# Modulation sums, query projections and inverse-transform quarters reordered around a 2-D attention stage, with a bias table that holds the mask

## Chip, core and metric

The kernel runs on one core of one Trainium2 chip. The metric is device time in microseconds of one execution. All times here are of that core: runs of the whole kernel, and one execution recorded by the hardware profiler, with its trace.

## What is computed

Two layers of a diffusion backbone over 512 tokens of width 1024, with 256 context tokens. Layer 0 mixes with a Hyena long convolution (512 channels) beside 2-D neighbourhood attention (8 heads of 64), layer 1 with a Conformer convolution; after each comes a ConvFFN of width 2816. Every sub-layer sits between RMS norms whose scale, shift and gate come from a conditioning vector (`m = silu(c) @ w_mod + b_mod`). The part that the change touches, cut from the reference:

```python
shift1, scale1, gate1, shift2, scale2, gate2 = adaln_params(c, w_mod[layer], b_mod[layer])
z = hn @ w_in[e]
y_hy = hyena_mixer(z[..., :3 * HY_WIDTH], ...)      # x0 * (irfft(rfft(x1*v) * k_f) + (x1*v) * bias)
q, k, v = jnp.split(z[..., 3 * HY_WIDTH:], 3, axis=-1)
...
s_loc = jnp.einsum('bjqhd,brjkhd->bhjqrk', q_blk, k_blk)     # 16 query columns x 8 rows of 32 key columns
s_loc = s_loc + bias.transpose(0, 2, 3, 1, 4)                # relative position table, per head
s_loc = jnp.where(col_ok[:, :, None, :], s_loc, NEG_BIG)     # -1e30 outside the window
s_ctx = jnp.einsum('bjqhd,bchd->bhjqc', q_blk, kc)
p = jax.nn.softmax(jnp.concatenate([s_loc, s_ctx], axis=-1), axis=-1)
y = jnp.concatenate([y_hy, y_na], axis=-1) @ w_out[e]
```

## The kernel before

Everything is fp32. A product of matrices is made of three matmuls on high and low parts (`mm3`, L296 to L299). Weights come by a stream: SP loads a tile of 128 x 1024 (512 KB) into one of three `raw` buffers (L308), ScalarE casts its high half (L314), VectorE subtracts for the low half (L315); the halves lie in `w` tiles, eight buffers. `s` tiles (31 buffers) hold nearly all else, and PSUM has eight banks (`ps`).

The program is written as one sequence, and a scheduler, which simulates a timeline as it builds, settles each engine's order from it; each engine then works strictly in its own order, and SP issues loads in its own.

The stages around the change, in layer 0:

- key projection: `k_proj` (L962), whose pieces kX and kcX are written by ScalarE and VectorE (L975, L976);
- forward transform: `fdft` (L982) makes four sums of products in PSUM (pv); its `prod` (L992) forms v0 and v1 (L998 to L1001), multiplies them by the filter K (one product on POOL, L1007, one on VectorE, L1008), combines (L1011, L1012) and splits the result into Eh and El (L1017, L1019). It runs twice;
- value projection: six accumulators va (L1045 on), copied to V; `v_shift` (L1072) copies shifted rows by DMA;
- inverse transform, in four quarters of 128 channels (py, L1081 on), each followed by two VectorE operations (L1096, L1098) that end in yh;
- query projection: `q_proj` (L1104), four of them; pz, then qX and qL (L1118, L1119);
- attention: 16 blocks u, four for each pair of heads. For each u the loop (L1224) calls scores (sc), exponent (L1172 on VectorE: score plus bias table BM, with the negative row maximum; then ScalarE), normalizing one block later (reciprocals on VectorE L1179, scaling on POOL L1180), transposes of P (pt) and their copies three blocks later, products with V (po) five later.

The bias table comes by `bm_load` (768 columns a head, L1131, with a memset of the context part, L1130), and `bm_make` adds the mask on POOL (L1135).

Beside this run background generators, of which `bg_step(n)` (L501) advances n steps wherever the code calls it. `mod_cols(0, (2,))` is one: it sums 16 tiles of `wcol`, each scaled by one number per partition, into `acc`, then eight small matmuls (pm, L465) reduce it to the second norm's scale and shift. With `side=True`, as here, ScalarE scales (L446) and POOL adds (L448); without it, VectorE does both in one operation (L452).

Of the kernel before, what the change touches and what calls it, by code (L numbers as in the profile page):

```python
# [29 lines left out]
def shape_constants():  # L30
    f64 = np.float64
    k = np.arange(256)
    t = np.arange(512)
    th = np.outer(2 * k + 1, 2 * t + 1) % 4096
    C = np.cos(th * (np.pi / 2048))
    S = np.sin(th * (np.pi / 2048))

    tf = np.zeros((4, P, 2, 256))
    for par in range(2):
        for hf in range(2):  # L40
            tt = 2 * (128 * hf + np.arange(128)) + par
# [36 lines left out]

    kb = [0, 8, 32]
    mask = np.zeros((P, 3, 4, 8, 8))  # L80
    s2, c8 = np.meshgrid(np.arange(2), np.arange(8), indexing="ij")
    for i, j in enumerate((0, 1, 3)):
        for s in range(2):
            for c in range(8):
                qc = 16 * j + 8 * s + c
                ws = min(max(qc - 8, 0), 48)
                kc = kb[i] + 8 * np.arange(4)[:, None] + np.arange(8)[None, :]
                ok = (kc >= ws) & (kc < ws + 16)
                m = np.where(ok, 0.0, -1e30)
                for r in range(8):  # L90
                    mask[s * 64 + r * 8 + c, i] = m[:, None, :]
    mask = mask.reshape(P, 768)

    kk = np.arange(128)
    w = np.pi * (2 * kk + 1) / 256
    tl = np.arange(256)
    ca = np.cos(np.outer(tl, w))
    sa = np.sin(np.outer(tl, w))
    f4 = np.zeros((4, P, 2, 128))
    for i, (lo, keep) in enumerate(((0, (0, 256)), (128, (0, 256)), (128, (0, 241)), (0, (15, 256)))):  # L100
        loc = lo + np.arange(128)
        on = ((loc >= keep[0]) & (loc < keep[1]))[:, None]
        f4[i, :, 0] = ca[loc] * on
        f4[i, :, 1] = sa[loc] * on
    f4 = f4.transpose(1, 0, 2, 3).reshape(P, 1024)
    i4 = np.zeros((4, P, 2, 128))
    for i, (lo, keep) in enumerate(((0, (0, 128)), (128, (0, 64)), (0, (64, 128)), (128, (0, 128)))):
        loc = lo + np.arange(128)
        on = ((np.arange(128) >= keep[0]) & (np.arange(128) < keep[1]))[None, :]
        i4[i, :, 0] = ca[loc].T * on / 128.0  # L110
        i4[i, :, 1] = sa[loc].T * on / 128.0
    i4 = i4.transpose(1, 0, 2, 3).reshape(P, 1024)
    j = np.arange(31)
    k31 = np.concatenate([np.cos(np.outer(j - 15, w)), np.sin(np.outer(j - 15, w))], 1)
    out = dict(tf=tf, ti=ti, cst=cst, zT=zT, dec=dec, qrow=q, mask=mask, f4=f4, i4=i4, k31=k31)
    return {n: np.ascontiguousarray(a.astype(np.float32)) for n, a in out.items()}


# [14 lines left out]
def layout(inp):  # L133
# [58 lines left out]
    a["fw3"] = g["hy_f_w3"][0]  # L192
    a["fw4"] = g["hy_f_w4"][0]

    rpb = g["na_rpb"][0]
    pad = np.concatenate([np.zeros_like(rpb[:, :, :17]), rpb, np.zeros_like(rpb[:, :, :17])], 2)
    tab = []
    for s in range(2):
        for r in range(8):
            for c in range(8):  # L200
                rows = pad[:, 7 - r:15 - r]
                per = []
                for off in (15, 7, -1):
                    b = 17 + off - (8 * s + c)
                    seg = rows[:, :, b:b + 32].reshape(8, 8, 4, 8).transpose(0, 2, 1, 3)
                    per.append(seg)
                tab.append(np.stack(per, 1))
    a["rpb"] = np.stack(tab, 1).reshape(8, P, 768)
    a.update(shape_constants())
    return {k: np.ascontiguousarray(v) for k, v in a.items()}, cols  # L210

# [41 lines left out]
def backbone_kernel(ctx: ExitStack, tc: tile.TileContext, a, cols, out, dump=None, stop=None, mark=lambda s: None):  # L253
# [76 lines left out]
    def flat(ap, pat):  # L330
        return ap.rearrange(pat)
# [96 lines left out]

    MOD = {}

    def gemv_acc(src, n, cs, init=None, side=False):
        rs = []

        def ld(k):
# [5 lines left out]
        for k in range(n):  # L440
            if k < n - 1:
                ld(k + 1)
            ck_ = cs[:, k:k + 1]
            if side:
                t_ = acc if k == 0 else s4(F32, (P, 1024), "gt")
                A.activation(t_, rs[k], AF.Copy, bias=0.0, scale=ck_)  # L446
                if k:
                    G.tensor_tensor(acc, acc, t_, op=ALU.add)  # L448
            elif k == 0 and init is None:
                V.tensor_scalar(acc, rs[k], ck_, None, op0=ALU.mult)  # L450
            else:
                V.scalar_tensor_tensor(acc, rs[k], ck_, init if k == 0 else acc, op0=ALU.mult, op1=ALU.add)  # L452
            yield acc

    def mod_cols(l, whichs, side=False):

        n = 2 * len(whichs)
        acc = None
        for acc in gemv_acc(a[f"wcol{l}"], 8 * n, scn[n], side=side):
            yield  # L460
        for _ in range(8):
            yield
# [488 lines left out]
                ctx_T()  # L951
        V.tensor_tensor(pp[i // 2][:, i % 2], got[0], got[1], op=ALU.mult)
    bg_drain()
    bg += [mod_cols(0, (2,), True)]


    mark("kproj")
# [24 lines left out]
    def fdft(fc):  # L982
# [9 lines left out]
        def prod():  # L992
# [10 lines left out]
            for pr, v in ((0, v0), (1, v1)):  # L1003
                kt = K[(fc, pr)]
                yy = s4(n="yy")
                tm = od if pr else s4(n="ytm")
                G.tensor_tensor(tm, v, kt[:, 1:2].broadcast_to([P, 2, 512]), op=ALU.mult)  # L1007
                V.tensor_tensor(yy, v, kt[:, 0:1].broadcast_to([P, 2, 512]), op=ALU.mult)  # L1008
                y.append((yy, tm))
            for yy, tm in y:  # L1010
# [9 lines left out]
            E[fc] = (eh, el)  # L1020
        return prod

    bg_step(3)
    ev0 = k_proj(0)
    p_T(3)
    bg_step(3)
    ev0()
    ev1 = k_proj(1)
    ev1()
    bg_step(3)  # L1030
    pr0 = fdft(0)
    pr0()
    mark("fdft")
    ev2 = k_proj(2)
    ev2()
    bg_step(3)
    ev3 = k_proj(3)
    ev3()
    bg_step(3)
    pr1 = fdft(1)  # L1040
    pr1()
    bg_step(3)


    mark("vproj")  # L1045
# [2 lines left out]
    for kp in range(4):  # L1048
# [11 lines left out]
                mm3(vacc[c], ah, al, wh[:, ns], wl[:, ns], kc == 0, kc == 7)  # L1060
        if kp in (1, 2):
            TI[kp - 1] = split(load(a["ti"][kp - 1]), None)
        bg_step(3)

    Vt = {}
    for c in range(6):
# [13 lines left out]

    mark("inv")  # L1081
    yh = [s4(n="yh") for _ in range(2)]
    for m in range(4):
        py = ps("py")
        ms = slice(m * P, (m + 1) * P)
        for par in range(2):
            o = py[:, par * 256:(par + 1) * 256]
            for fc in range(2):
                for cs in range(2):
# [6 lines left out]
        V.scalar_tensor_tensor(pi.rearrange("p (i e) -> p i e", e=2), pi.rearrange("p (i e) -> p i e", e=2),  # L1096
                               pc("hyb", m), py.rearrange("p (e i) -> p i e", e=2), op0=ALU.mult, op1=ALU.add)
        V.tensor_tensor(yh[m // 2][:, m % 2], pi, x0[m // 2][:, m % 2], op=ALU.mult)  # L1098

    mark("qproj")  # L1100

# [16 lines left out]
                A.mul(t_[HALF[r], e], src, 0.125)  # L1118
            V.scalar_tensor_tensor(l_[HALF[e], e], src, 0.125, f(t_[HALF[e], e]), op0=ALU.mult, op1=ALU.subtract)  # L1119

    q_proj(0)
    bg_step(1)

    mask = w4(F32, (P, 1024), "mask")
    SP.dma_start(mask[:, 0:768], a["mask"])
    BM = {}

    def bm_load(hd):
        BM[hd] = w4(F32, (P, 4, 256), "BM")
        G.memset(BM[hd][:, 3], 0.0)  # L1130
        SP.dma_start(flat(BM[hd][:, 0:3], "p a b -> p (a b)"), a["rpb"][hd])  # L1131

    def bm_make(hd):
        b = flat(BM[hd][:, 0:3], "p a b -> p (a b)")
        G.tensor_tensor(b, b, mask[:, 0:768], op=ALU.add)  # L1135

    for hd in range(2):
        bm_load(hd)
    q_proj(1)
    for hd in range(2):  # L1140
        bm_make(hd)
    bg_step(1)
    dmp("p", pT[0])
    dmp("x0", x0[0])
    dmp("yh", yh[0])

    mark("att")
    KS = (0, 1, 3, 4)
# [65 lines left out]
    def a_out(hp):  # L1214
# [5 lines left out]
        A.copy(hi, src)  # L1220
        V.tensor_tensor(lo, src, f(hi), op=ALU.subtract)

    DN, DT, DV = 1, 3, 5
    for u in range(16 + DV + 1):  # L1224
        if u < 16:
            a_scores(u)
            a_exp(u)
        if 2 <= u < 4:
            q_proj(u)
        if DN <= u < 16 + DN:  # L1230
            a_norm(u - DN)
        if DT <= u < 16 + DT:
# [3 lines left out]
            a_pv(u - DV)  # L1236
        if u > DV and (u - DV) % 2 == 0:
            a_out((u - DV) // 2 - 1)
        if u == 2:
            v_shift()  # L1240
        if u % 4 < 2 and u < 12:
            bm_load(u // 4 * 2 + u % 4 + 2)
        if u % 4 in (1, 2) and u < 12:
            bm_make(u // 4 * 2 + u % 4 + 1)
    dmp("yA", yA[0])
    mix.close()

# [302 lines left out]
```

## Time and profile before

| | us |
|---|---|
| median of 3 runs | 1291.08 |
| lowest and highest | 1290.09, 1294.53 |
| the profiled execution | 1290.61 |
| its span in the trace | 1288.8 |
| TensorE busy | 1249.9 (97%) |
| VectorE, ScalarE, POOL busy | 817.3 (63%), 526.8 (41%), 160.2 (12%) |

The mean granted clock of TensorE is 0.994 of full speed, and 171.00 MB move by DMA. The names of the trace are: PE for TensorE's matmuls, PEld for its weight loads, DVE for VectorE, ACT for ScalarE, POOL for GpSimd, SP for SyncE. Times in the trace count from the start of the span. A row "A <- B" in the list of waits says what an engine waited for, with the total, the number and the longest.

### The profile page before, as it was taken

To read this page: it belongs to the slowest core of one execution; us is meant where nothing else is said; L and a number is where in the kernel's file an instruction comes from. 1 tells how busy PE (TensorE), PEld (TensorE's weight loads), DVE (VectorE), ACT (ScalarE), POOL (GpSimd) and SP (SyncE) were. 2 spreads that over 40 slices of the span, in tenths; PEclk is the share of its full clock that TensorE was granted. 3 is DMA by queue.
4 is the path that set the end of the run, shared out by engine and by line. 5 is a ranking of instruction groups with operands and counts; after the bars stand their busy time and mean duration, and the time that the engine had idled before them with its cause. 6 is when DMAs were issued, how large, how long until landed. Compare 5 with 4: busy or idle time off the path is not lost.

```text
span 1288.8 us, 15592 instructions
## 1 busy us (share of the span) xinstructions
PE 1249.9 (97%) x6044; PEld 1027.3 (80%) x6044; DVE 817.3 (63%) x1068; ACT 526.8 (41%) x804; POOL 160.2 (12%) x198
## 2 busy tenths in 40 slices
PE   6999979999999999999999999999999999999997
PEld 3688867877898888878888887878888888888886
DVE  4577588476557888877825565686677555556233
ACT  5453543286435333243514433242544333345221
POOL 3210365283010000000000100101100000000001
PEclk9999998999999999999999999999999999999999
DMA  9536533342506477766336052040255333232321
GB/s 354 179 115 181 162 115 131 129 121 83 163 1 190 169 230 244 237 210 207 107 105 196 25 185 73 1 147 1 66 167 187 98 94 95 98 97 99 98 83 65
DMA packets 47818, 171.00 MB, mean 133 GB/s; under 512 B 5757, under 2 KB 5788, under 8 KB 47744
## 3 DMA queue, kind: packets, MB, share of 16 engines
q1 hardware_dynamic: 47092, 168.49, 39.9%
q0 software_dynamic: 464, 1.19, 0.4%
q8 instruction: 47, 0.77, 0.2%
q10 hardware_dynamic: 188, 0.33, 0.1%
q14 instruction: 27, 0.22, 0.1%
HBM read 167.10 MB, written 2.10 MB: 131 GB/s over the span
## 4 chain that ended last, share of the span: by engine, by line
PE 76%; DMA 8%; DVE 7%; ACT 4%; issue 3%; POOL 1%; SPq 0%; DVEq 0%; POOLq 0%; ACTq 0%
PE pz L297 12%; PE pz L298 12%; PE pz L299 12%; PE acc L297 8%; PE acc L298 8%; PE acc L299 8%; DMA raw<-in_wup 3%; DMA raw<-in_wcol 3%; DVE w L315 2%; PE pg L297 2%; PE pg L298 2%; PE pg L299 2%; ACT w L314 2%; PE po L1206 1%; PE pt L1186 1%
## 5 line engine op out<-in xcount | busy, mean ns | idle before, releaser
L299 PE MATMUL pz<-hTh,w 128*128 128x512 f32 (+1 forms) x920 | 345.2, 376 | 0.5 <-DVE w L315 0.5
L297 PE MATMUL pz<-hTh,w 128*128 128x512 f32 (+1 forms) x920 | 344.6, 377 | 0.9 <-DVE hTh L543 0.5
L298 PE MATMUL pz<-hTl,w 128*128 128x512 f32 (+1 forms) x920 | 345.4, 376 | 0.0
L315 DVE TENSOR_TENSOR w<-raw,w 128x1024 fp32r<-128x1024 f32 x159 | 201.1, 1268 | 211.1 <-ACT w L314 206.8
L314 ACT CAST w<-raw 128x1024 fp32r<-128x1024 f32 x159 | 166.3, 1051 | 345.5 <-PE pz L298 128.6
L299 PEld LDWEIGHTS pz<-hTh,w 128*128 128x128 f32 x920 | 173.8, 189 | 32.2 <-DVE w L315 1.0
L297 PEld LDWEIGHTS pz<-hTh,w 128*128 128x128 f32 x920 | 173.0, 189 | 31.5 <-DVE hTh L543 1.0
L298 PEld LDWEIGHTS pz<-hTl,w 128*128 128x128 f32 x920 | 173.9, 189 | 30.2 <-DVE hTl L544 0.4
L298 PE MATMUL acc<-w,gs 128*128 128x512 f32 x256 | 99.6, 389 | 0.0
L299 PE MATMUL acc<-w,gs 128*128 128x512 f32 x256 | 98.3, 389 | 0.0
L297 PE MATMUL acc<-w,gs 128*128 128x512 f32 x256 | 97.0, 389 | 0.0
L452 DVE SCALAR_TENSOR_TENSOR acc<-raw,sc,acc 128x1024 f32<-128x1024 f32 x59 | 75.6, 1281 | 28.6 <-DMA raw<-in_wgate 19.6
L416 POOL TENSOR_SCALAR t<-t,t 128x1 f32<-128x1 f32 x19 | 6.6, 348 | 636.6 <-ACT py L425 628.2
L901 ACT ACTIVATE cv<-pz,pk 128x512 f32<-128x512 f32 x88 | 67.6, 774 | 0.0
L903 DVE SCALAR_TENSOR_TENSOR cv<-pz,pk,cv 128x511 f32<-128x511 f32 x88 | 65.6, 747 | 1.8
L902 DVE SCALAR_TENSOR_TENSOR cv<-pz,pk,cv 128x511 f32<-128x511 f32 x88 | 65.2, 744 | 0.2 <-ACT cv L901 0.2
L1283 ACT ACTIVATE cv<-cv 128x512 f32<-128x512 f32 x44 | 27.7, 629 | 81.2 <-DVE cv L903 81.1
L297 PEld LDWEIGHTS acc<-w,gs 128*128 128x128 f32 x256 | 48.1, 188 | 10.1
L299 PEld LDWEIGHTS acc<-w,gs 128*128 128x128 f32 x256 | 48.1, 188 | 9.9
L298 PEld LDWEIGHTS acc<-w,gs 128*128 128x128 f32 x256 | 48.1, 188 | 9.9
L315 DVE TENSOR_TENSOR wk<-raw,wk 128x1024 fp32r<-128x1024 f32 x30 | 37.1, 1246 | 28.9 <-ACT wk L314 28.9
L558 DVE TENSOR_TENSOR py<-acc,gg 128x512 f32<-128x512 f32 x32 | 21.8, 688 | 48.4 <-ACT py L425 48.4
(334 smaller groups left out, 2050.2 us busy)
## 6 DMA issues: line engine op xcount, KB each, us to landing
raw<-in_wup SPq DMA_DIRECT2D x88, 512.0 KB, 3.6
raw<-in_wcol SPq DMA_DIRECT2D x48, 512.0 KB, 4.4
raw<-in_wdn SPq DMA_DIRECT2D x44, 512.0 KB, 3.6
raw<-in_wgate SPq DMA_DIRECT2D x32, 512.0 KB, 4.3
raw<-in_pw SPq DMA_DIRECT2D x24, 512.0 KB, 4.7
raw<-in_win SPq DMA_DIRECT2D x20, 512.0 KB, 3.6
land<-in_wmod SPq DMA_DIRECT2D x16, 512.0 KB, 10.2
raw<-in_wout SPq DMA_DIRECT2D x8, 512.0 KB, 3.6
```

The costliest lines, as they stand in the source:

```text
L297: PE.matmul(o, ah, bh, start=start, stop=False)
L298: PE.matmul(o, ah, bl, start=False, stop=False)
L299: PE.matmul(o, al, bh, start=False, stop=stop)
L314: A.copy(hi, r)
L315: V.tensor_tensor(lo, r, f(hi), op=ALU.subtract)
L452: V.scalar_tensor_tensor(acc, rs[k], ck_, init if k == 0 else acc, op0=ALU.mult, op1=ALU.add)
L558: V.tensor_tensor(p_[:, sl], y2[i], gg[:, sl], op=ALU.mult)
L901: A.activation(dst, pz, AF.Identity, bias=pc(bk, i), scale=pc(wk + "1", i))
L902: V.scalar_tensor_tensor(dst[:, 1:w], pz[:, 0:w - 1], pc(wk + "0", i), dst[:, 1:w], op0=ALU.mult, op1=ALU.add)
L903: V.scalar_tensor_tensor(dst[:, 0:w - 1], pz[:, 1:w], pc(wk + "2", i), dst[:, 0:w - 1], op0=ALU.mult, op1=ALU.add)
L1186: PE.transpose(b["pt"][:, c * P:(c + 1) * P], b["P"][:, c * P:(c + 1) * P], ident)
L1283: A.activation(cv[:, 0], cv[:, 0], AF.Silu, bias=0.0, scale=1.0)
```

## The change

Five things change. The second norm's modulation sums are made by VectorE, not by ScalarE and POOL. The product L1007 moves from POOL to VectorE. The calls of `bg_step` are fewer in the projections and transforms, and some stand in the inverse quarters and the attention loop. Query projections and inverse quarters take turns, the last two inside the first two rounds of the attention loop. The bias table is laid out on the host with the mask and the zeros of the context part, 1024 columns a head, so the mask's load, its sums and the memsets go.

```diff
-            if side:
-                t_ = acc if k == 0 else s4(F32, (P, 1024), "gt")
-                A.activation(t_, rs[k], AF.Copy, bias=0.0, scale=ck_)
-                if k:
-                    G.tensor_tensor(acc, acc, t_, op=ALU.add)
-            elif k == 0 and init is None:
+            if k == 0 and init is None:
                 V.tensor_scalar(acc, rs[k], ck_, None, op0=ALU.mult)
             else:
                 V.scalar_tensor_tensor(acc, rs[k], ck_, init if k == 0 else acc, op0=ALU.mult, op1=ALU.add)
...
-                G.tensor_tensor(tm, v, kt[:, 1:2].broadcast_to([P, 2, 512]), op=ALU.mult)
+                V.tensor_tensor(tm, v, kt[:, 1:2].broadcast_to([P, 2, 512]), op=ALU.mult)
...
-    bg_step(3)
+    bg_step(2)
     ev0 = k_proj(0)
     p_T(3)
-    bg_step(3)
+    bg_step(1)
     ev0()
     ev1 = k_proj(1)
     ev1()
-    bg_step(3)
     pr0 = fdft(0)
     pr0()
...
     for kp in range(4):
...
-        bg_step(3)
+        bg_step(1)
...
-    for m in range(4):
+
+    def inverse(m):
...
         V.tensor_tensor(yh[m // 2][:, m % 2], pi, x0[m // 2][:, m % 2], op=ALU.mult)
+        bg_step(2)
...
     def bm_load(hd):
         BM[hd] = w4(F32, (P, 4, 256), "BM")
-        G.memset(BM[hd][:, 3], 0.0)
-        SP.dma_start(flat(BM[hd][:, 0:3], "p a b -> p (a b)"), a["rpb"][hd])
...
+        SP.dma_start(flat(BM[hd], "p a b -> p (a b)"), a["rpb"][hd])
...
+    q_proj(0)
+    inverse(0)
+    for hd in range(2):
+        bm_load(hd)
+    q_proj(1)
+    inverse(1)
+    v_shift()
     DN, DT, DV = 1, 3, 5
     for u in range(16 + DV + 1):
         if u < 16:
             a_scores(u)
             a_exp(u)
-        if 2 <= u < 4:
-            q_proj(u)
+        if u < 2:
+            q_proj(u + 2)
+            inverse(u + 2)
+        bg_step(1)
...
-        if u == 2:
-            v_shift()
-        if u % 4 < 2 and u < 12:
-            bm_load(u // 4 * 2 + u % 4 + 2)
         if u % 4 in (1, 2) and u < 12:
-            bm_make(u // 4 * 2 + u % 4 + 1)
+            bm_load(u // 4 * 2 + u % 4 + 1)
```

How the engines' orders move shows at three places. The first is VectorE at the products of the first forward transform (yy, ytm and od are products, v their inputs, K the filter; w the low half of a weight). Before:

```order
L1008 TENSOR_TENSOR yy_1388<-v_279_1382,K_387 128x1024
L1008 TENSOR_TENSOR yy_1392<-v_280_1383,K_419 128x1024
L1011 TENSOR_TENSOR yy_1388<-yy_1388,ytm_1389 128x512
L1012 TENSOR_TENSOR yy_1388<-yy_1388,ytm_1389 128x512
L976 TENSOR_TENSOR kX_1469<-pz_1419,kX_1469 64x512
L315 TENSOR_TENSOR w_1494<-raw_1275,w_1493 128x1024
L976 TENSOR_TENSOR kcX_1172<-px_1420,kcX_1172 64x256
```

And now, with `acc` the modulation sum:

```order
L430 SCALAR_TENSOR_TENSOR acc_1173<-raw_1446,sc_122,acc_1173 128x1024
L977 TENSOR_TENSOR v_266_1350<-pv_1340,od_1347 128x512
L979 TENSOR_TENSOR v_267_1351<-pv_1340,od_1347 128x512
L985 TENSOR_TENSOR ytm_1357<-v_266_1350,K_387 128x1024
L986 TENSOR_TENSOR yy_1356<-v_266_1350,K_387 128x1024
L985 TENSOR_TENSOR od_1347<-v_267_1351,K_419 128x1024
L986 TENSOR_TENSOR yy_1360<-v_267_1351,K_419 128x1024
```

A modulation step stands among the sums v, and the two products of POOL stand beside VectorE's own.

The second place is SP's queue from the transform tables (in_ti) on. Before:

```order
L308 DMA raw_1739<-in_ti 128x1024
L308 DMA raw_1749<-in_win 128x1024
L308 DMA raw_1787<-in_ti 128x1024
L308 DMA raw_1812<-in_win 128x1024
L308 DMA raw_2016<-in_wout 128x1024
L1125 DMA mask_2004<-in_mask 128x768
L1131 DMA BM_2006<-in_rpb 128x768
```

And now:

```order
L291 DMA raw_1729<-in_ti 128x1024
L291 DMA raw_1735<-in_wcol 128x1024
L291 DMA raw_1742<-in_win 128x1024
L291 DMA raw_1780<-in_wcol 128x1024
L1105 DMA BM_1862<-in_rpb 128x1024
L1105 DMA BM_1864<-in_rpb 128x1024
L291 DMA raw_1856<-in_wcol 128x1024
L291 DMA raw_1859<-in_wcol 128x1024
L291 DMA raw_1870<-in_wout 128x1024
L291 DMA raw_1934<-in_wcol 128x1024
L291 DMA raw_1937<-in_wcol 128x1024
```

Column tiles (in_wcol) of the modulation now stand between the last weights, the bias tables and the first output weights.

The third place is VectorE ahead of the reciprocals of attention's second block (P is a block's exponent input, L1133; the reciprocals are L1140). Before (L1172 and L1179 there):

```order
L1172 ISA P_2087,t_2093<-sc_2078,BM_2009 128x512
L1172 ISA t_2093 128x1
L1119 SCALAR_TENSOR_TENSOR qL_2044<-pz_2018,qX_2043 64x512
L1179 RECIPROCAL t_2096<-t_2066 128x1
L1179 RECIPROCAL t_2099<-t_2067 128x1
```

And now:

```order
L298 TENSOR_TENSOR w_2064<-raw_1870,w_2063 128x1024
L430 SCALAR_TENSOR_TENSOR acc_1173<-raw_2038,sc_122,acc_1173 128x1024
L1133 ISA P_2150,t_2153<-sc_2140,BM_1862 128x512
L1133 ISA t_2153 128x1
L1075 TENSOR_TENSOR yh_1793<-p_626,x_145_624 128x512
L1098 SCALAR_TENSOR_TENSOR qL_2095<-pz_2069,qX_2094 64x512
L1155 COPY PT_2202<-pt_2197 128x4x128
L1133 ISA P_2150,t_2156<-sc_2141,BM_1864 128x512
L1133 ISA t_2156 128x1
L1098 SCALAR_TENSOR_TENSOR qL_2095<-pz_2069,qX_2094 64x512
L1140 RECIPROCAL t_2159<-t_2055 128x1
L1140 RECIPROCAL t_2162<-t_2056 128x1
```

Modulation steps, inverse quarters and low halves of the query now stand ahead of these reciprocals.

## Rows read from the trace of the kernel before

**Rows 1.** The page's busy time of TensorE: us, share of the span, instructions.

```profile
PE 1249.9 (97%) x6044; PEld 1027.3 (80%) x6044; DVE 817.3 (63%) x1068; ACT 526.8 (41%) x804; POOL 160.2 (12%) x198
```

**Rows 2.** Waits of TensorE, 150 to 520 us: total, times, longest.

```profile
PE va L297 <- ACT w L314: 5.1, 1, 5.1
PE va L298 <- DVE w L315: 3.8, 1, 3.8
PE py L297 <- ACT w L314: 2.1, 1, 2.1
PE pt L1186 <- POOL P L1180: 1.7, 2, 0.9
...
PE py L298 <- DVE w L315: 0.9, 1, 0.9
```

**Rows 3.** Windows: length; PE, PEld, DVE, ACT, POOL busy; PEclk; DMA share; GB/s.

```profile
135.00:240.00 105.00, 91.31 (x449) 76.51 (x448) 73.31 (x73) 46.84 (x63) 51.02 (x21) 0.93 0.41 133
190.00:195.00 5.00, 1.14 (x2) 0.42 (x2) 4.94 (x4) 3.53 (x5) 3.27 (x2) 0.58 0.19 78
195.00:200.00 5.00, 4.47 (x11) 3.50 (x12) 3.24 (x5) 1.19 (x2) 0.00 (x0) 0.50 0.64 233
200.00:205.00 5.00, 5.00 (x21) 4.09 (x20) 2.48 (x4) 2.56 (x4) 4.45 (x2) 0.90 0.87 285
235.00:240.00 5.00, 5.00 (x31) 5.00 (x31) 2.66 (x3) 2.05 (x4) 0.00 (x0) 0.66 0.47 148
```

**Rows 4.** Groups of VectorE, 135 to 330 us: busy, mean ns; idle before, releaser.

```profile
L315 DVE TENSOR_TENSOR w<-raw,w 128x1024 fp32r<-128x1024 f32 x15 | 25.4, 1702 | 20.0 <-ACT w L314 16.1 <-PE pz L298 3.8
...
L1008 DVE TENSOR_TENSOR yy<-v,K 128x1024 f32<-128x1024 f32 x4 | 11.0, 2770 | 0.6 <-POOL acc L448 0.6
L1017 DVE TENSOR_TENSOR v<-yy,yy 128x512 f32<-128x512 f32 x8 | 9.4, 1231 | 0.0
...
L315 DVE TENSOR_TENSOR wk<-raw,wk 128x1024 fp32r<-128x1024 f32 x4 | 4.7, 1219 | 2.6 <-ACT wk L314 2.6
...
L1098 DVE TENSOR_TENSOR yh<-p,x 128x512 f32<-128x512 f32 x4 | 2.8, 692 | 0.2
```

**Rows 5.** Groups of POOL, 135 to 330 us.

```profile
L448 POOL TENSOR_TENSOR acc<-acc,gt 128x1024 f32<-128x1024 f32 x15 | 38.5, 2570 | 85.0 <-ACT gt L446 84.6
L1180 POOL TENSOR_SCALAR P<-P,t 128x512 f32<-128x512 f32 x32 | 22.8, 727 | 14.4 <-DVE t L1179 11.9 <-PE pt L1186 2.4
```

**Rows 6.** The page's group of VectorE's scaled sums, whole span.

```profile
L452 DVE SCALAR_TENSOR_TENSOR acc<-raw,sc,acc 128x1024 f32<-128x1024 f32 x59 | 75.6, 1281 | 28.6 <-DMA raw<-in_wgate 19.6
```

**Rows 7.** The page's DMA issues: KB each, median us from issue to landing.

```profile
raw<-in_wcol SPq DMA_DIRECT2D x48, 512.0 KB, 4.4
...
raw<-in_win SPq DMA_DIRECT2D x20, 512.0 KB, 3.6
```

**Rows 8.** Timeline of VectorE: start, duration, [wait before it and its releaser].

```profile
165.76 0.69 DVE L998 TENSOR_TENSOR v<-pv,od 128x512 f32<-128x512 f32 x1 [4.00 <-POOL acc L448]
...
212.05 1.21 DVE L1008 TENSOR_TENSOR yy<-v,K 128x1024 f32<-128x1024 f32 x1
```

**Rows 9.** Timeline of TensorE.

```profile
182.49 0.50 PE L297 MATMUL va<-w,hTh 128*128 128x512 f32 x1 [1.39 <-DVE kX L976]
...
220.18 1.95 PE L465 MATMUL pm<-sel,acc 128*128 128x2 f32 x16 [0.49 <-POOL acc L448]
...
230.27 0.28 PE L297 MATMUL py<-w,Eh 128*128 128x256 f32 x1
...
268.20 0.36 PE L1159 MATMUL sc<-kX,qX 128*128 128x256 f32 x1
...
269.12 0.28 PE L1160 MATMUL sc<-kcX,qL 128*128 128x256 f32 x1
...
274.26 1.04 PE L1186 MATMUL pt<-ident,P 128*128 128x128 f32 x8
```

**Rows 10.** The chain of waits, 135 to 200 us: start, duration.

```profile
137.82 5.92 DMA raw<-in_wcol
```

More of the change, by code (lines that the diff above doesn't have):

```diff
@@ L77, in shape_constants @@
     q = np.exp(-deltas / 511.0)[None, :]
[L79 to L92, printed above, removed]
     kk = np.arange(128)
@@ L114, in shape_constants @@
     k31 = np.concatenate([np.cos(np.outer(j - 15, w)), np.sin(np.outer(j - 15, w))], 1)
-    out = dict(tf=tf, ti=ti, cst=cst, zT=zT, dec=dec, qrow=q, mask=mask, f4=f4, i4=i4, k31=k31)
+    out = dict(tf=tf, ti=ti, cst=cst, zT=zT, dec=dec, qrow=q, f4=f4, i4=i4, k31=k31)
     return {n: np.ascontiguousarray(a.astype(np.float32)) for n, a in out.items()}
@@ L195, in layout @@
     rpb = g["na_rpb"][0]
[L196 to L199, printed above, removed]
+    tab = np.full((8, 2, 8, 8, 3, 8, 32), -1e30, np.float32)
+    for i, (j, kb) in enumerate(((0, 0), (1, 8), (3, 32))):
+        for s in range(2):
             for c in range(8):
[L201 to L208, printed above, removed]
+                qc = 16 * j + 8 * s + c
+                w0 = min(max(qc - 8, 0), 48)
+                for r in range(8):
+                    tab[:, s, r, c, i, :, w0 - kb:w0 - kb + 16] = rpb[:, 7 - r:15 - r, w0 - qc + 15:w0 - qc + 31]
+    tab = tab.reshape(8, P, 3, 8, 4, 8).transpose(0, 1, 2, 4, 3, 5).reshape(8, P, 768)
+    a["rpb"] = np.concatenate([tab, np.zeros((8, P, 256), np.float32)], 2)
     a.update(shape_constants())
@@ L429, in backbone_kernel, with gemv_acc @@
     MOD = {}
-    def gemv_acc(src, n, cs, init=None, side=False):
+    def gemv_acc(src, n, cs, init=None):
         rs = []
@@ L453, in gemv_acc, with mod_cols @@
             yield acc
-    def mod_cols(l, whichs, side=False):
+    def mod_cols(l, whichs):
         n = 2 * len(whichs)
         acc = None
-        for acc in gemv_acc(a[f"wcol{l}"], 8 * n, scn[n], side=side):
+        for acc in gemv_acc(a[f"wcol{l}"], 8 * n, scn[n]):
             yield
@@ L953, in backbone_kernel @@
     bg_drain()
-    bg += [mod_cols(0, (2,), True)]
+    bg += [mod_cols(0, (2,))]
     mark("kproj")
@@ L1035, in backbone_kernel @@
     ev2()
-    bg_step(3)
+    bg_step(1)
     ev3 = k_proj(3)
     ev3()
-    bg_step(3)
+    bg_step(1)
     pr1 = fdft(1)
     pr1()
-    bg_step(3)
     mark("vproj")
@@ L1062, in backbone_kernel @@
             TI[kp - 1] = split(load(a["ti"][kp - 1]), None)
-        bg_step(3)
+        bg_step(1)
     Vt = {}
@@ L1119, in q_proj @@
             V.scalar_tensor_tensor(l_[HALF[e], e], src, 0.125, f(t_[HALF[e], e]), op0=ALU.mult, op1=ALU.subtract)
[L1121 to L1125, printed above, removed]
     BM = {}
@@ L1129, in bm_load @@
         BM[hd] = w4(F32, (P, 4, 256), "BM")
-        G.memset(BM[hd][:, 3], 0.0)
-        SP.dma_start(flat(BM[hd][:, 0:3], "p a b -> p (a b)"), a["rpb"][hd])
[L1133 to L1145, printed above, removed]
+        SP.dma_start(flat(BM[hd], "p a b -> p (a b)"), a["rpb"][hd])
     mark("att")
@@ L1227, in backbone_kernel @@
             a_exp(u)
-        if 2 <= u < 4:
-            q_proj(u)
+        if u < 2:
+            q_proj(u + 2)
+            inverse(u + 2)
+        bg_step(1)
         if DN <= u < 16 + DN:
```

## Prediction

> **What bounds the kernel.** I read the page's busy table first: TensorE is busy for 97% of the span [rows 1], so only idle time and half-clock time of TensorE can be won. The list of TensorE's waits for 150 to 520 us, which covers all that the diff touches, shows where that is: the value projection (tile va) waits 5.1 and 3.8 us for split weights, the inverse transform (py) 2.1 and 0.9 us for the same, and the transposes of attention (pt) 1.7 us for POOL [rows 2]. Two waits of the same stretch stand in the timeline: 1.39 us for kX ahead of the first va product and 0.49 us for POOL's sum ahead of pm [rows 9]. The windows show what follows an idle stretch: from 195 to 200 us TensorE is granted 0.50, the lower of its two levels (1.2 of 2.4 GHz), and 0.58, 0.90 and 0.66 in three slices beside idle stretches [rows 3].
>
> Why are the weights late? They are not late from memory. VectorE, which makes their low halves, takes 1702 ns for each in 135 to 330 us, against 1219 ns for the same operation on wk; its product L1008 takes 2770 ns on average, and 1.21 us in the timeline where POOL had just finished [rows 4, 8]; POOL meanwhile adds 1024 columns for 2570 ns each [rows 5]. So the two engines slow each other. VectorE also waits 4.00 us for POOL's sum before its first sum v at 165.76 [rows 8].
>
> **What goes, by the trace.** If VectorE comes in time, the value projection gives back 1.4 + 5.1 + 3.8 + 0.5 = 10.8 us and the inverse 2.1 + 0.9 = 3.0. The half-clock share costs half of the busy time at that level: 1.14 x 0.42 + 4.47 x 0.50 + 5.00 x 0.10 + 5.00 x 0.34 = 4.9 [rows 3]. Together 18.7. The 1.7 of attention's transposes I leave: scaling by POOL stays as it is.
>
> **What VectorE gets.** Sixteen modulation steps, each at the 1281 ns of L452 [rows 6], 20.5 us; four products moved from POOL at 1.21 [rows 8], 4.8 us; together 25.3. What it is given: L1008 4 x (2.77 - 1.21) = 6.2; low halves 15 x (1.70 - 1.22) = 7.2; L1017 8 x (1.23 - 0.69) = 4.4 [rows 4]; the wait of 4.00 [rows 8]; together 21.8. So VectorE's account is about even, though 73.31 of 105 us were busy [rows 3]. ScalarE loses 16 activations and POOL 15 sums, masks and memsets; neither bounds the stretch, so I cost that at nothing beyond the above. Moving the mask into the table adds 128 KB to each of eight loads and removes one load: hidden, as no wait for BM stands in [rows 2]. The turns of query projections and inverse quarters give TensorE the same products in another order, with 24 projection products as cover for each quarter's weights.
>
> A rule speaks against the move: the Trainium skill, "Perfetto Trace Analysis", section "Optimizing Scalar/DVE Operations", says that a saturated VectorE may gain from handing work to ScalarE or GPSIMD, and that a port shared with GPSIMD may spoil it. By its first half, the sum would carry 25 us more of VectorE and lose the gain. The trace bears out its second half here: 1.21 against 2.77 for one product.
>
> **Is VectorE in time for the value projection?** It could start its sums at 165.76 - 4.00 = 161.8 [rows 8]. In the change one modulation step stands in between, and to the last kX follow some 14.3 us: four sums of 0.6 (they start closer than the 0.69 that each lasts), four products 4.8, four combinations of 0.6, one low half 1.2, kX and kcX pieces 2.2, the modulation step 1.3 and 1.2 more of a low half. So 176.1, and TensorE comes at 182.49 - 1.39 = 181.1 [rows 9]. The next banks need 8.6 us more of VectorE (184.7), TensorE some 6.8 us of products later (187.9). Margin 3 to 5 us: the waits go.
>
> **The new wait.** VectorE's order puts, between the value projection and block 1's reciprocals, the modulation steps that before ran on POOL. Each load of a column tile gets its raw buffer only when VectorE has consumed the one before; SP issues in order, so the steps are a chain of round trips, a landing L plus 1.28 each. Behind them on VectorE stand exponent inputs P, low halves of q and the reciprocals; POOL's scaling and TensorE's transposes of block 1 follow, in order, with all later blocks.
>
> TensorE unhindered is at these transposes at 274.26 - 18.7 - 1.95 (pm comes later in the new order) = 253.6 [rows 9]. The value projection ends where py began, 230.27, less 10.8 of waits, 3.2 of half clock and 1.95 of pm: 214.3. One copy, cast and low half, 2.9 (estimate: the low half at 1.22 [rows 4], the others at less), give 217.2 for the start of the chain, which has seven round trips. After it come six half-width operations and a reciprocal, some 4.45 (0.69 each [rows 4]), and POOL's 0.73 [rows 5].
>
> L is not to be seen in that place before. The nearest rows: 3.6 median of in_win, 4.4 median of in_wcol [rows 7], 5.92 the longest column tile on the chain [rows 10]. I take 4.0, between the medians, as SP's queue is less loaded here than at the kernel's start, where most column tiles land. Then 217.2 + 7 x 5.28 = 254.2, + 4.45 + 0.73 = 259.3: **TensorE waits 5.7 us**. At 4.4 it is 8.5, at 5.92 it is 19.1. The lower end does not depend on loads: the last quarter's products end at about 249.6 (three blocks of scores of some 1.0 each, from 268.20 to past 269.12 in the trace, and 1.04 of transposes ahead of the wait [rows 9]); the sum behind them (0.75), a low half, a modulation step, 4.45 and 0.73 give 258.1, a wait of 4.5. After the wait the clock: as after the 3.0 us of waits at 230 to 235 us, 5.00 x 0.34 = 1.7 [rows 3]; at most the 3.2 of the longer one.
>
> **Sum.** -18.7 + 5.7 + 1.7 = -11.3, against the profiled execution's 1290.61: 1279.3. The median of the three runs is 0.47 above it, so **1279.8**.
>
> **Rivals.**
> 1. *Round trips hidden, faster still.* If loads run ahead (L near or below 3.6), the wait is the floor of 4.5 and the clock is kept: 1291.08 - 18.7 + 4.5 = 1276.9, 1275.2 if attention's 1.7 go as well, and a margin of 1 below that. For: the queue has little else to do, 0.41 of the DMA engines [rows 3]. Against: seven in a row, each with its own buffer wait.
> The Trainium skill, "SBUF — State Buffer", section "The DMA setup-cost knee", gives a fixed 2 us plus bytes at 436 GB/s: an estimate of 3.2 us for 512 KB, which by itself would make this rival the likeliest. The rows have 3.6 at least for a median [rows 7], and the measurement decides.
> 2. *VectorE late again.* If its operations in the value projection stay as slow as the low halves are now (1.70 for 1.22, a factor 1.4), 14.3 becomes 20.0 and the next 8.6 becomes 12: 181.8 and 193.8, the second 5.9 past TensorE's 187.9. With 1.3 of half clock again, 1279.8 + 7.2 = 1287. For: VectorE is busy almost without a gap there (4.94 of 5.00 at 190 us [rows 3]). Against: what slows it, POOL's operations, is gone from this stretch. It is also how the change could fail to do what it says: the work goes to VectorE and no wait goes.
> 3. *Slower: the chain of column tiles.* At L = 5.92 for each, as the longest on the chain, the wait is 19.1 and the clock 3.2: -18.7 + 22.3 = +3.6, so 1294.7. It decides from L = 5.4 (seven times 1.4 is 9.8 more than forecast; with 1.5 of clock that eats the 11.3). For: two bias loads and output weights share SP's queue with the tiles. Against: it needs every landing to be as long as the longest.
>
> **Chances.** Forecast 0.64, rival 1 0.14, rival 2 0.13, rival 3 0.09. 0.3% of the time is 3.9 us, about what can be told from no change. Faster (below 1287.2): the forecast with L up to about 4.9, rival 1 and half of rival 2: 0.80. Same: the other half, and the forecast at L near 5.2: 0.12. Slower: the rest, 0.08. The range: from 1274 (rival 1's end) to 1288 (past rival 2, L about 5.0); it leaves out rival 3 and the tails, some 0.17.
>
> **What would show it.** Right: no va or py wait for split weights over 1 us; full clock from 180 to 210 us; the product lines at 1.2 us; a wait of pt for POOL's P of 4 to 7 us at block 1, with VectorE's modulation steps waiting for landings of in_wcol before it; the end of the value projection near 214. Wrong: va waiting for VectorE or kX (rival 2); a pt wait near 20 us (rival 3); no pt wait above 5 (rival 1); or a stall at a place that the sum does not have, such as SP's in-order queue holding back wout's weights.

## The result

The changed kernel takes 1277.06 us (median of 4 runs, 1275.65 to 1277.40), against 1290.59 for the one before on the same chip (4 runs): a ratio of 0.9889, 95% interval 0.9865 to 0.9913. The profiled execution took 1276.72 with a span of 1274.9, against 1290.61 and 1288.8. The forecast was 1279.8, its range 1274 to 1288.

TensorE's waits from 150 to 520 us, which answer to [rows 2], are now two:

```profile
PE pt L1147 <- POOL P L1141: 4.7, 1, 4.7
PE pz L280 <- DVE hTh L521: 0.3, 1, 0.3
```

The waits of the value projection and of the inverse transform are gone, and so are the two of 0.9 us ahead of attention's transposes. The forecast's new wait has come, at the transposes of block 1. The windows that answer to [rows 3] (same columns):

```profile
190.00:195.00 5.00, 5.00 (x24) 4.14 (x23) 5.00 (x7) 0.71 (x1) 0.00 (x0) 1.00 0.37 117
195.00:200.00 5.00, 5.00 (x24) 4.14 (x23) 4.95 (x8) 3.11 (x6) 1.88 (x4) 1.00 0.36 105
200.00:205.00 5.00, 5.00 (x24) 4.14 (x23) 3.75 (x5) 0.37 (x1) 0.21 (x1) 1.00 0.57 174
...
250.00:255.00 5.00, 2.88 (x23) 2.51 (x22) 4.71 (x7) 3.27 (x7) 0.18 (x1) 1.00 1.02 416
255.00:260.00 5.00, 2.41 (x11) 2.41 (x12) 4.88 (x16) 3.67 (x9) 2.95 (x4) 0.53 0.95 347
260.00:265.00 5.00, 5.00 (x41) 4.53 (x42) 4.04 (x17) 3.75 (x9) 2.80 (x5) 0.79 0.64 252
```

From 190 to 205 us TensorE is full and at full clock. The idle time has moved to 250 to 260, and the clock falls there: 2.41 x 0.47 + 5.00 x 0.21 = 2.2 us lost. VectorE's groups, 135 to 330 us, which answer to [rows 4], have no slow operation left:

```profile
L298 DVE TENSOR_TENSOR w<-raw,w 128x1024 fp32r<-128x1024 f32 x19 | 23.3, 1228 | 12.6 <-ACT w L297 12.4
L430 DVE SCALAR_TENSOR_TENSOR acc<-raw,sc,acc 128x1024 f32<-128x1024 f32 x15 | 19.2, 1282 | 17.6 <-DMA raw<-in_wcol 17.6
...
L995 DVE TENSOR_TENSOR v<-yy,yy 128x512 f32<-128x512 f32 x8 | 5.1, 687 | 0.1
...
L986 DVE TENSOR_TENSOR yy<-v,K 128x1024 f32<-128x1024 f32 x4 | 4.9, 1219 | 0.0
```

1228 ns for 1702, 687 for 1231, 1219 for 2770. And the timeline of TensorE has the last product of the value projection, block 1's transposes, the first products of the output projection, and the first of the ConvFFN's down projection:

```profile
213.28 0.39 PE L282 MATMUL va<-w,cT 128*128 128x512 f32 x1
...
257.59 1.97 PE L1147 MATMUL pt<-ident,P 128*128 128x128 f32 x8 [4.72 <-POOL P L1141]
...
305.99 0.50 PE L280 MATMUL acc<-w,yH 128*128 128x512 f32 x1
...
601.81 0.39 PE L280 MATMUL acc<-w,gs 128*128 128x512 f32 x1
```

Before, the same four are at 230.05, 274.26 [rows 9], 322.17 and 616.05:

```profile
322.17 0.50 PE L297 MATMUL acc<-w,yH 128*128 128x512 f32 x1
...
616.05 0.39 PE L297 MATMUL acc<-w,gs 128*128 128x512 f32 x1
```

So 16.8 us are won by the end of the value projection (1.95 of them because pm comes later), 16.2 by the end of attention, but only 14.2 at the down projection and 13.9 in the whole span: some 2 us are given back between the output projection and the down projection, in the first ConvFFN.

What ended the wait at block 1 shows in the chain of waits (start, length, what):

```profile
237.73 3.53 DMA raw<-in_wcol
...
241.36 1.28 DVE acc L430
...
249.31 0.95 ACT w L297
...
251.44 1.29 DVE acc L430
...
256.52 0.22 DVE t L1140 x2
...
256.85 0.70 POOL P L1141
...
257.59 0.48 PE pt L1147
```

One landing of 3.53 us stands on this stretch of the chain. From 241.36 on it is VectorE's own work with ScalarE's copies and casts between: modulation steps, low halves, exponent inputs, then the reciprocals, as its order put them. The forecast had two limits for this place, the round trips of the modulation steps and the work behind the last inverse quarter's products (py). VectorE's timeline shows that they met there (each row's bracket is the wait before it and what ended it):

```profile
248.96 0.75 DVE L1073 SCALAR_TENSOR_TENSOR p<-p,pk,py 128x512 f32<-128x512 f32 x1 [0.36 <-PE py L282]
...
250.28 1.23 DVE L298 TENSOR_TENSOR w<-raw,w 128x1024 fp32r<-128x1024 f32 x1 [0.58 <-ACT w L297]
```

VectorE stood idle for 0.36 us until the last products of the quarter were done, and for 0.58 us until a cast. Yet the seven modulation steps from 221.49 on followed each other every 5.0 us, close to the forecast's 5.28, and the seventh ran from 251.44 to 252.73, where the forecast had 254.2. When the seventh tile landed is not in the trace, so this trace doesn't say which of the two limits was the later one.

### The profile page after: what moved, and what is told of

Same layout as the page of the kernel before. It is cut to its first block, busy times and chain, and to the rows that moved or that the text cites. A ratio compares the mean times of both kernels' runs of the same rounds, so it can differ in the third digit from the quotient of the medians.

```text
span 1274.9 us, 15534 instructions
## 1 busy us (share of the span) xinstructions
PE 1245.7 (98%) x6044; PEld 1025.7 (80%) x6044; DVE 816.8 (64%) x1088; ACT 509.6 (40%) x788; POOL 94.4 (7%) x163
## 4 chain that ended last, share of the span: by engine, by line
PE 81%; DMA 7%; DVE 7%; ACT 2%; issue 2%; POOL 1%; DVEq 0%; POOLq 0%; SPq 0%; ACTq 0%
PE pz L280 11%; PE pz L281 11%; PE pz L282 11%; PE acc L282 8%; PE acc L280 8%; PE acc L281 8%; DMA raw<-in_wcol 3%; DMA raw<-in_wup 3%; PE pg L280 2%; PE pg L281 2%; PE pg L282 2%; DVE acc L430 2%; DVE w L298 2%; PE po L1167 1%; PE pt L1147 1%
## 5 line engine op out<-in xcount | busy, mean ns | idle before, releaser
L298 DVE TENSOR_TENSOR w<-raw,w 128x1024 fp32r<-128x1024 f32 x159 | 194.1, 1223 | 200.9 <-ACT w L297 200.2
L430 DVE SCALAR_TENSOR_TENSOR acc<-raw,sc,acc 128x1024 f32<-128x1024 f32 x74 | 94.8, 1281 | 47.3 <-DMA raw<-in_wcol 27.7
```

What stands on the lines that cost most here:

```text
L298: V.tensor_tensor(lo, r, f(hi), op=ALU.subtract)
```

## The experiments

All twelve runs with their medians and the ratio to the kernel before on the same chip ("last va": start of the last value projection product, 230.05 before; TensorE's waits over 1 us from 150 to 520 us):

| run | us | ratio, 95% interval | last va | waits |
|---|---|---|---|---|
| the change | 1277.06 | 0.9889 (0.9865 to 0.9913) | 213.3 | pt 4.7 |
| e1 sums by ScalarE and POOL | 1290.38 | 1.0002 (0.9987 to 1.0016) | 213.5 | pt 10.3, pz 3.2 and 1.1 |
| e2 ScalarE and VectorE | 1286.20 | 0.9970 (0.9960 to 0.9981) | 214.4 | pt 6.8, pz 5.1 |
| e3 POOL alone | 1285.13 | 0.9967 (0.9954 to 0.9980) | 214.9 | pt 15.2 |
| e4 products on POOL | 1282.57 | 0.9936 (0.9914 to 0.9958) | 213.5 | pt 5.5, pz 1.9 and 1.2 |
| e5 before, VectorE sums | 1280.88 | 0.9916 (0.9898 to 0.9934) | 217.5 | py 3.3, pt 2.4 |
| e11 before, sums and products | 1274.13 | 0.9861 (0.9836 to 0.9886) | 216.9 | py 3.3, pt 2.1 |
| e9 before, thinned steps | 1294.40 | 1.0024 (1.0010 to 1.0037) | 214.6 | sc 18.1, py 1.8 and 1.4 |
| e12 before, mask in the table | 1289.06 | 0.9973 (0.9957 to 0.9989) | 229.8 | va 5.1, 3.7, 1.5, py 2.4 |
| e6 no turns | 1271.91 | 0.9846 (0.9828 to 0.9865) | 214.4 | sc 1.8 |
| e8 steps early | 1275.12 | 0.9871 (0.9855 to 0.9888) | 213.6 | pz 2.2, pt 2.0, py 1.3 |
| e7 steps late | 1279.57 | 0.9900 (0.9879 to 0.9921) | 214.6 | pm 3.1, pt 2.5 |
| e10 no turns, steps late | 1277.79 | 0.9887 (0.9864 to 0.9911) | 214.0 | pm 2.8, pt 2.0 |

**Who makes the modulation sums.** Three kernels put them elsewhere and leave all else as changed. In e1 ScalarE scales and POOL adds, as before:

```diff
-            if k == 0 and init is None:
+            if side:
+                t_ = acc if k == 0 else s4(F32, (P, 1024), "gt")
+                A.activation(t_, rs[k], AF.Copy, bias=0.0, scale=ck_)
+                if k:
+                    G.tensor_tensor(acc, acc, t_, op=ALU.add)
+            elif k == 0 and init is None:
...
-    bg += [mod_cols(0, (2,))]
+    bg += [mod_cols(0, (2,), True)]
```

> The changed kernel (1277.06 us) with one part undone: the modulation sums of the second norm again scaled by ScalarE and added by POOL. Contention theory (mine: POOL's sums slow VectorE, and VectorE's sums wait behind POOL): low halves L298-like go from 1.22 us to 1.5 us or more on average in 135 to 330 us, 5 to 11 us of va waits and 2 to 5 us of half clock return: 1284 to 1293 us. Order theory (the turns of projections and inverse quarters and the thinner steps brought the gain): va waits stay under 2 us in all, 1276 to 1280 us.

Measured: 1290.38, the whole gain gone; low halves 1832 ns. But the last product of the value projection started at 213.5 with no wait before it; the time was lost later. The second half of the contention theory's expectation (va waits) missed. Of the chain of waits from 205 to 275 us, 40.1% are landings of column tiles.

In e2 ScalarE scales and VectorE adds (`V.tensor_tensor` for `G.tensor_tensor`), so POOL has no part:

> The changed kernel with the modulation tiles scaled by ScalarE and added by VectorE, POOL left out. Contention theory: low halves stay at 1.22 us, va waits under 2 us, 1276 to 1280 us (VectorE's add of two tiles costs what its one operation did). ScalarE-queue theory (before, ScalarE's copies od of the transform stood behind scalings that waited for a column tile's landing, and VectorE's first sums behind those): the sums v wait 3 to 4 us, va waits 3 to 8 us, 1281 to 1287 us.

Measured: 1286.20. Low halves were at 1225 ns, so nothing slowed VectorE, and still most of the gain was gone: the time that the ScalarE-queue theory gave, though not at the place that it named. The waits of TensorE, then of ScalarE from 135 to 240 us:

```profile
PE pt L1152 <- POOL P L1146: 6.8, 2, 5.0
PE pz L280 <- ACT w L297: 5.1, 1, 5.1
```

```profile
ACT gt L429 <- DMA raw<-in_wcol: 17.9, 6, 4.7
```

And the chain of waits behind them, from 234 us:

```profile
234.36 1.16 ACT gt L429
...
235.54 6.26 DMA raw<-in_wcol
...
241.88 1.15 ACT gt L429
```

ScalarE stands still until each column tile lands, and the casts, exponents and copies behind the scaling stand with it. Standing at landings alone is not what costs: in the changed kernel VectorE stands at them almost as long in the same window,

```profile
DVE acc L430 <- DMA raw<-in_wcol: 15.8, 7, 5.6
```

and TensorE doesn't wait for it before block 1. What differs is what comes behind in the queue, and ScalarE also has 16 scalings of some 1.16 us more to do in e2. How much of the loss is the standing and how much is this added work, no run separates.

In e3 POOL scales and adds (`G.tensor_scalar` in place of `A.activation`):

> The changed kernel with the modulation tiles both scaled and added by POOL, ScalarE left out. Contention theory: POOL is busy some 50 us in the stretch, low halves and products of VectorE slow down as in the kernel before (1.5 us and more, products 2 us and more where they overlap), va waits of 4 us or more return: 1281 to 1293 us. ScalarE-queue theory: nothing waits in ScalarE's queue, 1276 to 1280 us.

Measured: 1285.13, within contention's range: low halves 1509 ns, the v sums (L995 of the change) 1351 for 687. Again not as va waits: one wait of 14.6 us at the transposes. VectorE's slowing is only a part of what stands before that wait. On the chain there is one low half of 3.75 us, then a column tile's landing, and then POOL's own queue, in which the scaling of P comes behind a modulation sum (the chain's row, then POOL's timeline):

```profile
254.75 6.85 DMA raw<-in_wcol
```

```profile
264.01 2.33 POOL L431 TENSOR_TENSOR acc<-acc,gt 128x1024 f32<-128x1024 f32 x1
266.32 1.35 POOL L1146 TENSOR_SCALAR P<-P,t 128x512 f32<-128x512 f32 x2
```

So e3 does not isolate the slowing of VectorE by POOL: POOL's queue costs here as ScalarE's does in e2. By the ratios, the sums cost some 0.8% (10 us) on either engine, and 1.1% (14 us) on both together, in e1: the two costs do not add up.

**The products.** e4 puts the four products back on POOL:

```diff
-                V.tensor_tensor(tm, v, kt[:, 1:2].broadcast_to([P, 2, 512]), op=ALU.mult)
+                G.tensor_tensor(tm, v, kt[:, 1:2].broadcast_to([P, 2, 512]), op=ALU.mult)
```

> The changed kernel with the four products od and ytm back on POOL, the modulation sums staying on VectorE. Contention theory: VectorE's own products overlap POOL's and take 2.4 to 3.4 us instead of 1.22, some 1.5 us each for four, against 4 x 1.22 us that leave VectorE; the margin of 3 to 5 us at the value projection covers it: 1276 to 1279 us, va waits under 1.5 us. Rival (the products alone set when the weights come): va waits of 3 us or more, 1281 us or more.

Measured: 1282.57, above the contention theory's range and in the time that the rival gave, though the va waits that it named did not come. VectorE's own products took 2792 ns beside POOL's, the low halves 1349. The margin held where I had looked; but what was late came later: waits of pz for split weights (1.9 and 1.2) and more at attention's transposes.

**One part alone.** e5 is the kernel before with the sums on VectorE (`mod_cols(0, (2,))` without `True`), e11 is e5 with the products on VectorE as well:

> The kernel before with one part of the change alone: VectorE makes the modulation sums; three steps at each call, as before. Four runs of the changed kernel with parts undone all ended the value projection at 213.9 to 215.3 us (before 230.4), so it is open what brought that. Contention theory (which engine sums decides): va waits under 2 us, value projection ends at 214 to 218, 1276 to 1283 us. Thinning theory (how many modulation tiles stand among the key and value projections decides): 5 us or more of va waits stay, end at 222 or later, 1285 to 1292 us.

> The kernel before with the modulation sums and also the four products on VectorE, three steps a call, no turns, mask on the chip. It tells what the products add to the run with the sums alone (1280.88 us, value projection ending at 217.9 us). Contention theory: products 1.22 us instead of 2.31, low halves 1.22 instead of 1.35, end at 214 to 216, py waits of 4 us stay: 1276 to 1279.5 us. If VectorE becomes the limit (4.9 us more on it): end at 218 or later, 1281 us or more.

Measured: e5 1280.88, the last product of the value projection starting at 217.5, with VectorE's products still at 2314 ns; e11 1274.13, products at 1218. e11 is faster than its range, though its value projection ended at 217.2, later than expected. Its ratio, 0.9861, is that of the whole change within the intervals: the two moves to VectorE alone carry the gain. The products' share of it is some 0.5% (e11 against e5, and the change against e4). The waits left in e11 are those that the other parts of the change remove:

```profile
PE py L297 <- ACT w L314: 3.3, 1, 3.3
PE pt L1186 <- POOL P L1180: 2.1, 2, 1.2
```

e9 is the kernel before with the steps thinned as in the change (2 and 1 for 3 in the projections, 1 per value step, 2 per quarter, 1 per attention round), sums still by ScalarE and POOL:

> The kernel before with only the modulation steps thinned as in the change (and the rest of them in the inverse quarters and the attention loop); ScalarE and POOL still make the sums, products on POOL, no turns. Thinning theory: value projection ends at 213 to 217, va waits under 2 us; the steps left over stand ahead of attention, where transposes wait 5 to 10 us for POOL: 1280 to 1291 us. Contention theory: va waits of 5 us or more stay, value projection ends after 222, 1287 us or more.

Measured: 1294.40, above the range of the thinning theory and a little slower than the kernel before. The value projection ended at 215.0, as thinning has it, and everything came back ahead of attention, not at the transposes for POOL but in one wait of the scores of 17.5 us for ScalarE, and in seven landings of column tiles on the chain between 218 and 258 us. The wait, and two of the landings:

```profile
PE sc L1156 <- ACT qX L1117: 18.1, 2, 17.5
```

```profile
234.21 3.49 DMA raw<-in_wcol
...
238.91 3.73 DMA raw<-in_wcol
```

So the postponed modulation tiles cost no less here than where they had stood, as long as ScalarE and POOL made the sums. e12 is the kernel before with the mask in the table:

> The kernel before with only the mask moved into the bias table (no mask load, no memsets and no sums on POOL). Forecast's view: costs and brings nothing, 1287 to 1292 us, pt waits 1 to 2 us. Rival (POOL's 14.7 us of mask sums delay its scaling of P, which the transposes wait for): pt waits go and 2 to 4 us are won, 1285 to 1288 us.

Measured: 1289.06, inside the forecast's range in us, but the ratio, 0.9973 (0.9957 to 0.9989), says 3.5 us less on that chip, and the transposes' wait for POOL (1.7 in [rows 2]) is no longer in the list. That is the rival's mechanism. POOL's timeline in the kernel before shows it: a mask sum, and right behind it the scaling whose transposes waited at 281.71 and 284.85:

```profile
279.16 1.83 POOL L1135 TENSOR_TENSOR BM<-BM,mask 128x768 f32<-128x768 f32 x1 [1.98 <-DMA BM<-in_rpb]
280.96 1.37 POOL L1180 TENSOR_SCALAR P<-P,t 128x512 f32<-128x512 f32 x2
282.28 1.84 POOL L1135 TENSOR_TENSOR BM<-BM,mask 128x768 f32<-128x768 f32 x1
284.10 1.37 POOL L1180 TENSOR_SCALAR P<-P,t 128x512 f32<-128x512 f32 x2
```

**The turns and the steps.** e6 undoes the turns:

```diff
+    for m in range(4):
+        inverse(m)
     q_proj(0)
-    inverse(0)
...
-        if u < 2:
-            q_proj(u + 2)
-            inverse(u + 2)
+        if 2 <= u < 4:
+            q_proj(u)
```

> The changed kernel without the turns: four inverse quarters one after the other, then the query projections, the last two in the attention loop as before. Forecast's view (the turns only cover the split of the inverse's weights): py waits of 2 to 3 us and their half clock come back, the pt wait of 4.7 us shrinks as yh and q come earlier: 1276 to 1281 us. Rival (the turns set when attention's first blocks can run): pt waits under 2 us, and the py wait is smaller than what that wins: 1272 to 1275 us.

Measured: 1271.91, the lowest median of all, though by the ratios the intervals of e6 and e11 overlap. No py wait came back: with fewer steps the table weights are split in time anyway. The output projection starts at 305.96, against 305.99 with the turns, so up to there the turns bring nothing and cost nothing. The profiled execution of e6, 1274.56, is the slowest of its four, so the trace shows only 2.4 us of a lead of some 5. Of these, 1.9 arise between there and the ConvFFN's down projection, 293.9 us against 295.8: there the change waits four times for split weights (1.7 us together), e6 twice (0.9). First the change, then e6, rows of TensorE's timeline:

```profile
525.91 0.50 PE L282 MATMUL pz<-hTh,w 128*128 128x512 f32 x1 [0.45 <-DVE w L298]
531.49 0.50 PE L280 MATMUL pz<-hTh,w 128*128 128x512 f32 x1 [0.29 <-ACT w L297]
532.75 0.50 PE L282 MATMUL pz<-hTh,w 128*128 128x512 f32 x1 [0.53 <-DVE w L298]
538.90 0.50 PE L282 MATMUL pz<-hTh,w 128*128 128x512 f32 x1 [0.40 <-DVE w L298]
```

```profile
536.26 0.50 PE L280 MATMUL pz<-hTh,w 128*128 128x512 f32 x1 [0.36 <-ACT w L297]
537.52 0.50 PE L282 MATMUL pz<-hTh,w 128*128 128x512 f32 x1 [0.53 <-DVE w L298]
```

These waits make up less than half of the 1.9 us. The code of that stage is the same in both; the scheduler orders it from its simulated timeline, which differs. That this is the cause was not tried.

e8 moves the quarters' steps into the value projection (three at each of its four calls, none in `inverse`), e7 puts them at two a round from attention's round 3 on, e10 does that to e6:

> The changed kernel with the two modulation steps of each inverse quarter moved into the value projection (three steps at each of its four calls, none in the quarters). Floor theory (the pt wait of 4.7 us is VectorE's own work behind the last inverse quarter): the wait falls to 1.8 to 3.5 us, 1273 to 1276 us. Round-trip theory (loads of column tiles set it): under 1.5 us, 1271 to 1274 us. Thinning theory: twelve steps in the value projection bring its waits back, 3 us or more of va waits, 1279 us or more.

> The changed kernel with no modulation step in the inverse quarters or the first three attention rounds; from round 3 on two steps a round. Floor theory (the pt wait of 4.7 us is VectorE's own work behind the last inverse quarter, of which one step of 1.28 us and the work piled up ahead of it go): pt wait 1.8 to 3.5 us, 1271 to 1275.5 us. Round-trip theory (landings of column tiles set it): the wait falls under 1.5 us, 1269 to 1272 us. A new wait from twelve steps inside attention would show as pt or sc waits at later blocks, 1276 us or more.

> The run without turns (1271.91 us), with the modulation steps of the inverse quarters moved to two a round from attention's round 3 on. If the steps are what delays the query's low halves there (sc waits of 1.8 and 0.6 us and 3.3 us of half clock): those go, 1266 to 1270 us. If the late steps crowd attention instead: pt or sc waits of 2 us or more at later blocks, 1271 to 1275 us.

Measured: e8 1275.12 with a pt wait of 2.0, e7 1279.57 with one of 2.5, e10 1277.79, above both of its ranges. By their ratios none of the three is told apart from the change. Both pt waits of e7 and e8 lie where the floor theory put them and not below the 1.5 us of the round-trip theory. So 2 us or more of the wait are not round trips; but 2.2 and 2.7 us of it went, more than the one step of 1.28 us that the floor has in it, and what the rest was is open. What e7 and e10 won there they lost elsewhere, in a wait that I had not named: pm, the matmuls that reduce the sums, stands in the middle of TensorE's attention order and waits for the last sum (in e10 the profile names a reciprocal right behind that sum). In e7, where the windows after it have 0.54 and 0.78 of the clock:

```profile
284.16 2.41 PE L443 MATMUL pm<-sel,acc 128*128 128x2 f32 x16 [3.14 <-DVE acc L430]
```

## Why the prediction was right, and where it was off

The time came out 2.7 us below the forecast and inside the range. By its terms, against the profiled executions:

- *What goes, 18.7 us*: right. Every va, py and pm wait is gone and the clock is full at 190 to 205 us; the value projection ended at 213.3 + 0.4 = 213.7, forecast 214.3.
- *Why it goes*: half right. That the sums and products belong on VectorE is shown both ways: e5 and e11 bring the gain with these moves alone, e1 loses it without the sums'. As the reason the forecast had POOL and VectorE slowing each other. They do (low halves 1509 ns for 1228 in e3, products 2792 for 1219 in e4), and the products alone, moved away from POOL, are worth some 0.5%. But e2 loses 0.8% with no operation of VectorE slowed. Its chain shows what the forecast did not name: ScalarE's in-order queue at the scalings, behind landings of column tiles; in e3 it is POOL's queue. The trace of before had pointed to it: its scalings wait 13.5 us for column tiles from 135 to 240 us, and POOL's sums stand behind them [rows 5]. And e9 shows that the waits of the value projection alone were no measure of it: they can be emptied without VectorE, and come back as 18.1 us elsewhere. How the loss divides between the slowing and the queues stays open.
- *VectorE in time, margin 3 to 5 us*: right, no va wait; the first va product started at 180.87 without one. The working has a slip: the operations that it lists add up to 15.5 us, not 14.3, which makes 177.3 of 176.1 and takes 1.2 from both margins.
- *The new wait, 5.7 us*: 4.7, at the named place. The landing was mis-sized, 3.53 on the chain for the 4.0 taken; with the other terms of the chain a little shorter too, POOL's scaling was done 1.7 us earlier than forecast, and TensorE was there 0.7 earlier (252.9 for 253.6). The result lies at the forecast's floor of 4.5, and e7 and e8 show that 2 us or more of it stay without round trips, but the seven steps kept the forecast's pace to within 0.3 us each, so the floor alone is not shown to have set the wait. Rival 1's condition came half true: the landing was below 3.6, but the loads did not run ahead, since VectorE waited 15.8 us for them. Its 1276.9 is nearer than the forecast by luck, as the clock was not kept. The Trainium skill, "SBUF — State Buffer", section "The DMA setup-cost knee", gives an estimate of 3.2 us for this size; the landing in this trace, 3.53, is nearer to it than the 4.0.
- *Clock, 1.7 us*: 2.2. Rival 1 kept the clock; that part of it failed.
- *The mask, nothing*: failed. "Moving the mask into the table ... hidden" looked only for waits on BM. The mask sums stood in POOL's queue ahead of the scaling that the transposes wait for; without them the 1.7 us of [rows 2] went, in the change and in e12, while e5 and e11, which keep them, have 2.4 and 2.1 there.
- *The end of the sum*: it stopped at attention. There the changed kernel was 16.2 us ahead (1.95 for pm included on both sides by then), forecast 11.3: of the 4.9, 1.7 are the transposes' waits and 0.5 is the smaller new wait (1.0) less the dearer clock (0.5); the other 2.7 are spread over attention and the value projection, and no single row accounts for them. Then 2.3 were given back, 1.9 of them in the first ConvFFN, which the forecast did not consider. So that the total came within 2.7 us is in part luck: two things that the sum left out went opposite ways.

The second rival (VectorE late) and the third (chain at 5.92) did not happen. The third's mechanism did in e2 and e9, where the tiles pass through ScalarE: there landings of 3.3 to 6.3 us stood on the chain one after the other.

The rule of the Trainium skill that spoke against the change ("Perfetto Trace Analysis", "Optimizing Scalar/DVE Operations": a saturated VectorE may gain from handing work over) did not decide here. VectorE was busy for 73.31 of 105 us [rows 3], and e5 and e11, which only add work to it, are 0.8% and 1.4% faster than before.

## What to carry to other kernels

When weights come late, ask of every side task not how busy its engine is but what stands behind it in each in-order queue: in e2 a scaling that waited for a load held up the casts behind it, and in e3 a sum held up POOL's scaling of P, whichever engine had time on average. A side task that is only postponed can show up again at the next tight place, as in e9, so judge it at the end of the whole stretch, not at the wait that it empties. And look at POOL's order, not only at the table's arrival, before calling a small POOL operation free.

## What was not expected of the hardware

A wait does not always cost clock. In e8 TensorE idled 2.00 us before block 1's transposes, and the windows around it stay at full clock (PEclk is the third number from the right):

```profile
255.00:260.00 5.00, 3.00 (x26) 2.66 (x24) 4.96 (x14) 3.83 (x9) 1.29 (x2) 1.00 1.02 411
260.00:265.00 5.00, 4.97 (x44) 3.96 (x44) 5.00 (x19) 4.64 (x13) 3.05 (x6) 1.00 0.77 302
```

In the change 4.72 us of idle time at that place were followed by 0.53 and 0.79, and before, 2.1 and 0.9 us close together by 0.66 [rows 3]. And the engines slow each other both ways. In e1 two of POOL's sums, some 2.4 us each when VectorE is quiet, took 11.50 together while VectorE worked through combinations, splits and two low halves with one pause of 0.70, and the two low halves, 1.22 each when POOL is quiet, took 5.98 (spans on POOL are rough, so 11.50 is a size and no exact number). VectorE's combinations and splits beside them kept their pace of 0.69 each, so it is not every operation that is slowed. POOL's rows, then VectorE's:

```profile
193.46 11.50 POOL L431 TENSOR_TENSOR acc<-acc,gt 128x1024 f32<-128x1024 f32 x2 [13.47 <-ACT gt L429]
...
207.92 2.40 POOL L431 TENSOR_TENSOR acc<-acc,gt 128x1024 f32<-128x1024 f32 x1 [2.96 <-ACT gt L429]
```

```profile
200.06 5.98 DVE L298 TENSOR_TENSOR w<-raw,w 128x1024 fp32r<-128x1024 f32 x2 [0.70 <-ACT w L297]
```
